# The first product of a gated feed-forward block in seven half-size products, with its result passed through HBM

## The chip, the cores and the metric

One core of one Trainium2 chip runs the whole layer. The metric is the device time of one execution in microseconds; three runs of the kernel before are shown, and one profiled execution of it is read.

## The reference, cut to what matters

The layer is a mixer block (state-space branch and windowed attention, untouched here) and then this, in float32 for 1,024 tokens behind 16 meta tokens:

```python
D_MODEL, D_FF, FFN_CONV = 1024, 2816, 3

def conv_ffn(h, norm_w, w_in, conv_w, conv_b, w_down):
    u = rmsnorm(h, norm_w)
    hid = causal_dwconv(u @ w_in.astype(u.dtype), conv_w, conv_b)   # (T,1024) @ (1024,5632)
    up, gate = jnp.split(hid, 2, axis=-1)
    return (jax.nn.silu(gate) * up) @ w_down.astype(h.dtype)        # (T,2816) @ (2816,1024)

h = h + valid_h * mixer_block(...)
h = h + valid_h * conv_ffn(h, ...)
y = rmsnorm(h, norm_final_w)
```

The convolution looks two tokens back along the sequence, so the first real token needs the last two meta tokens.

## The kernel before

Every large product keeps float32 accuracy by splitting both operands into a high part in TensorE's rounded float32 format and a remainder. The helper `split` (L93 to L95) does this: ScalarE copies the value into the high part, VectorE subtracts it from the value and writes the remainder. One product is then three matmuls per 128-deep slice of the contraction: high by high, high by remainder, remainder by high (L163 to L165 in `gemm_slice`).

Three stages at the end of the program matter here.

**Output projection** (L975 to L992). The nine token blocks are taken in the order 1, 2, 0, 3, 4, 5, 6, 7, 8 (block 0 holds two meta tokens, the others 128 tokens). For each block two PSUM banks of 512 columns take 24 matmuls each (L983 to L985), VectorE adds the residual into `hh` (L991), which stays in SBUF for all blocks, and `norm_T` (L173 to L186) normalises the block: a square with a running sum on ScalarE (L176), a small step on VectorE (L177), a power on GpSimd (L178), a scaling on VectorE (L179), eight transposes on TensorE (L184), and `split` into the two operand tiles `r1h_` and `r1l_` (1,024 deep, 1,040 tokens).

**First product of the feed-forward block** (L999 on). The 5,632 output channels are 44 jobs of 128 channels, a gate job and an up job in turn. Each job runs `gemm` over three token slices of 344, 344 and 342 columns (the list `SLF`), with 8 contraction steps of three matmuls: 72 matmuls. `conv3` (L1008 to L1016) applies the convolution straight from PSUM. The product of gate and up is split on the spot into `ah` and `al` and stays in SBUF. `prep` (L135 to L146) loads and splits the weights of the job two ahead, through the pool `wp` with three buffers `wf` and two each of `wh` and `wl`.

**Second product** (`down`, L1025 to L1058). As soon as three (or two) chunks of 128 channels are ready (list `G`), their part of the second product runs: 16 banks (8 token blocks by 2 halves) with three matmuls of 512 columns per chunk (L1044 to L1046), and VectorE adds each bank to `hh` (L1047). After the last group each block is normalised and stored.

A scheduler sets the order of the instructions on each engine; each engine runs its own list in that order, and the DMAs of this program are all issued from the SP queue, also in order.

## Time and profile before

| | |
|---|---|
| median of 3 runs | 2262.59 us (2261.64 to 2264.21) |
| the profiled execution, its own time | 2263.22 us |
| its span, first to last instruction | 2261.4 us |
| mean granted TensorE clock | 0.996 |
| TensorE busy | 2222.2 us, 98% of the span |
| VectorE, ScalarE, GpSimd busy | 1209.9, 817.7 and 181.5 us |
| start of the first matmul of the first product | 1504.67 us |
| start of the last matmul of the second product | 2254.09 us |

Times inside the span count from its start. Matmuls are pipelined, so the duration of one (0.32 us for 344 columns) is longer than the distance to the next; the distance from start to start is what a stream of them costs. A row of the timeline shows start, duration, engine, line, operation, output from inputs, shape and count, and, where the engine was idle before, for how long and what ended it. Some matmul records are missing from a trace, so stretches are counted by the code and not by the records.

### The profile page before, as it was taken

The page shows a single profiled execution, that of the slowest core. Times are in us where ns is not written, and L with a number is a line of the kernel's source. Part 1 is how long each engine was busy: PE and PEld are TensorE (multiplying, and loading weights), DVE is VectorE, ACT ScalarE, POOL GpSimd, SP SyncE. Part 2 cuts the span into 40 slices and gives each one's busy share as a digit, 9 for nine tenths or more (in the row PEclk, how much of TensorE's full clock was granted, in tenths as well). Part 3 has the DMA queues.
Part 4 walks back from the last instruction along what each step waited for, and adds up shares of the span by engine and source line. Part 5 has one row for each costly group of instructions (what it writes and reads, how often), then busy time and mean ns, then how long its engine had stood idle before and what let it go on. Part 6 is the DMA issues. An engine that isn't in the chain of part 4 may idle for free.

```text
span 2261.4 us, 34124 instructions
## 1 busy us (share of the span) xinstructions
PE 2222.2 (98%) x13546; PEld 2069.9 (92%) x13546; DVE 1209.9 (54%) x2349; ACT 817.7 (36%) x1696; POOL 181.5 (8%) x215
## 2 busy tenths in 40 slices
PE   7999999999999999999999999999999999999998
PEld 6899899998889988989999999789999898989997
DVE  6566554567665465365155545436354544545555
ACT  5445444446543443254222113223132231412333
POOL 1101110003320121031000000000000000000000
PEclk9999999999999999999999999999999999999999
DMA  6522421347643453375355434202020111211112
GB/s 180 121 61 65 112 69 52 96 129 162 153 127 109 131 151 94 95 163 171 100 180 164 116 94 139 97 20 75 19 66 29 56 38 47 63 32 47 57 38 75
DMA packets 286109, 214.38 MB, mean 95 GB/s; under 512 B 29592, under 2 KB 266034, under 8 KB 285439
## 3 DMA queue, kind: packets, MB, share of 16 engines
q1 hardware_dynamic: 285951, 212.21, 33.7%
q8 instruction: 107, 1.75, 0.3%
q14 instruction: 51, 0.42, 0.1%
HBM read 162.42 MB, written 49.74 MB: 94 GB/s over the span
## 4 chain that ended last, share of the span: by engine, by line
PE 92%; DMA 5%; DVE 2%; issue 0%; ACT 0%; SPq 0%; POOL 0%; DVEq 0%; POOLq 0%; ACTq 0%
PE gacc L164 21%; PE gacc L163 21%; PE gacc L165 21%; PE dacc L1044 4%; PE dacc L1046 4%; PE dacc L1045 4%; PE ssdyd L743 2%; PE attO L540 2%; DMA st<-g_d 2%; PE ssdst L730 1%; PE gacc L983 1%; PE gacc L984 1%; PE gacc L985 1%; PE ssdyo L725 1%; DMA att_k<-k_d 1%; PE ssdE L688 1%
## 5 line engine op out<-in xcount | busy, mean ns | idle before, releaser
L163 PE MATMUL gacc<-r1h,wh 128*128 128x342 f32 (+5 forms) x2832 | 919.3, 325 | 6.4 <-DVE cv L449 4.1
L164 PE MATMUL gacc<-r1l,wh 128*128 128x342 f32 (+5 forms) x2832 | 919.6, 325 | 2.2 <-DVE ss L177 1.5
L165 PE MATMUL gacc<-r1h,wl 128*128 128x342 f32 (+5 forms) x2832 | 918.3, 325 | 0.0
L163 PEld LDWEIGHTS gacc<-r1h,wh 128*128 128x128 f32 x2832 | 535.0, 189 | 15.0 <-issue 8.5
L164 PEld LDWEIGHTS gacc<-r1l,wh 128*128 128x128 f32 x2832 | 535.0, 189 | 10.7 <-issue 4.8
L165 PEld LDWEIGHTS gacc<-r1h,wl 128*128 128x128 f32 x2832 | 534.9, 189 | 6.2 <-issue 3.9
L95 DVE TENSOR_TENSOR wl<-wf,wh 128x1024 fp32r<-128x1024 f32 x117 | 144.4, 1234 | 179.2 <-ACT wh L94 177.7
L94 ACT ACTIVATE wh<-wf 128x1024 fp32r<-128x1024 f32 x135 | 142.1, 1053 | 209.8 <-PE gacc L164 183.6
L1047 DVE TENSOR_TENSOR hh<-dacc,hh 128x512 f32<-128x512 f32 x128 | 88.4, 691 | 122.2 <-PE dacc L1046 121.6
L449 DVE SCALAR_TENSOR_TENSOR cv<-gacc,cvw,cv 128x346 f32<-128x346 f32 (+2 forms) x216 | 123.8, 573 | 44.5 <-ACT cv L445 41.4
L1044 PE MATMUL dacc<-dh,ah 128*128 128x512 f32 x352 | 139.1, 395 | 0.0
L1045 PE MATMUL dacc<-dh,al 128*128 128x512 f32 x352 | 139.0, 395 | 0.0
L1046 PE MATMUL dacc<-dl,ah 128*128 128x512 f32 x352 | 139.0, 395 | 0.0
L1012 ACT ACTIVATE cg<-gacc,fcw 128x342 f32<-128x342 f32 (+1 forms) x66 | 41.5, 631 | 258.4 <-PE gacc L165 258.4
L163 PE MATMUL gacc<-r2h,wh 128*128 128x342 f32 x384 | 122.6, 319 | 3.5 <-DVE acc L913 2.4
L165 PE MATMUL gacc<-r2h,wl 128*128 128x342 f32 x384 | 122.8, 320 | 0.0
L164 PE MATMUL gacc<-r2l,wh 128*128 128x342 f32 x384 | 122.8, 320 | 0.0
L1015 DVE SCALAR_TENSOR_TENSOR cg<-gacc,fcw,cg 128x342 f32<-128x342 f32 x132 | 75.3, 572 | 68.4 <-ACT cg L1012 66.5
L1015 DVE SCALAR_TENSOR_TENSOR cu<-gacc,fcw,cu 128x342 f32<-128x342 f32 x132 | 75.4, 571 | 37.4 <-ACT cu L1012 35.3
L1046 PEld LDWEIGHTS dacc<-dl,ah 128*128 128x128 f32 x352 | 66.1, 188 | 16.0
L1044 PEld LDWEIGHTS dacc<-dh,ah 128*128 128x128 f32 x352 | 66.1, 188 | 15.2
L1045 PEld LDWEIGHTS dacc<-dh,al 128*128 128x128 f32 x352 | 66.1, 188 | 15.2
(334 smaller groups left out, 2917.6 us busy)
## 6 DMA issues: line engine op xcount, KB each, us to landing
wf<-in_w_in SPq DMA_DIRECT2D x66, 512.0 KB
wf<-in_w_ffn_in SPq DMA_DIRECT2D x44, 512.0 KB
gl<-ga_d SPq DMA_DIRECT2D x72, 171.0 KB
wf<-in_w_ffn_out SPq DMA_DIRECT2D x22, 512.0 KB
xs_d<-xt SPq DMA_DIRECT2D x16, 520.0 KB
z_d<-zt SPq DMA_DIRECT2D x16, 513.0 KB
ga_d<-gt SPq DMA_DIRECT2D x16, 513.0 KB
st<-g_d SPq DMA_DIRECT2D x48, 171.0 KB
```

What stands on the lines that cost most here:

```text
L94: act.activation(hi, src, AF.Copy)
L95: (eng or dve).tensor_tensor(out=lo, in0=src, in1=ff(hi), op=ALU.subtract)
L163: pe.matmul(ps[:m, :n], wh[:, k, :m], rh[k][:, t0:t0 + n], start=k == 0, stop=False)
L164: pe.matmul(ps[:m, :n], wh[:, k, :m], rl[k][:, t0:t0 + n], start=False, stop=False)
L165: pe.matmul(ps[:m, :n], wl[:, k, :m], rh[k][:, t0:t0 + n], start=False, stop=k == KC - 1)
L449: dve.scalar_tensor_tensor(out=t[:, z:m], in0=ps[:, off + z - lag:off + m - lag], scalar=w, in1=t[:, z:m], op0=ALU.mult, op1=ALU.add)
L540: pe.matmul(O[:, col:col + qn], at.v[:, kb - 1, o:o + P], pts[kb][:, e, q0:q0 + qn], start=False, stop=stop)
L1015: dve.scalar_tensor_tensor(out=t[:, :m], in0=ps[:, off - lag:off + m - lag], scalar=w, in1=t[:, :m], op0=ALU.mult, op1=ALU.add)
L1044: pe.matmul(ps, ah[:, tb], wh[:, cs], start=i == 0, stop=False)
L1045: pe.matmul(ps, al[:, tb], wh[:, cs], start=False, stop=False)
L1046: pe.matmul(ps, ah[:, tb], wl[:, cs], start=False, stop=i == len(grp) - 1)
L1047: dve.tensor_tensor(out=hh[:, b, cs], in0=ps, in1=hh[:, b, cs], op=ALU.add)
```

## The change

The channels of up chunk j and gate chunk j (two 128-channel blocks of the weight) and the two halves of the contraction (512 deep each) form a 2 by 2 block of weights; the two halves of the contraction and the two halves of the tokens (514 and 514 columns, with the two tokens ahead of each half included) form the other 2 by 2 block. Instead of eight half-size products, seven are made from sums and differences of the blocks, in Winograd's form of Strassen's scheme.

The activation sums T1 to T4 are made once, block by block, in the output projection (`sums`): T1 lies in the columns of `r1h_` and `r1l_` that the scheme does not need otherwise, T2 in a new tile, T3 and T4 are stored to HBM (`t_d`) and loaded back afterwards. The blocks are taken in the order 8, 4, 7, 3, 0, 6, 2, 5, 1, since block b and block b + 4 must meet. The residual `hh` no longer stays in SBUF; it is stored to HBM (`h_d`). The weight sums S1 to S4 are made for each j on GpSimd (`wprep`). The product of gate and up is stored to HBM (`a_d`), and the second product is a stage of its own that loads and splits it again (`parts`), with a first group of one chunk and seven of three.

```diff
-    hh = hp.tile([P, NB, D], F32, name="hh")
+    X2 = [xp.tile([P, 4, HT], F32R, name=f"x2{i}") for i in range(2)]
...
+        def sums(t0, n, b11, b21, b12, b22, t3, tz):
...
+            dve.tensor_tensor(out=t1, in0=b12, in1=b11, op=ALU.subtract)
+            split(*col(0, t0, n), b11)
+            split(*col(1, t0, n), b21)
+            dve.tensor_tensor(out=t2, in0=b22, in1=t1, op=ALU.subtract)
+            split(*col(4, t0, n), t2)
+            split(*col(3, t0, n), t1)
+            dve.tensor_tensor(out=t4, in0=b21, in1=t2, op=ALU.subtract)
+            for i, t in enumerate((t3, t4)):
+                z = [q[:, 4 * i:4 * i + 4, :n] for q in tz]
+                split(*z, t)
+                for j in range(2):
+                    sp.dma_start(t_d[i, j][:, :, t0:t0 + n], ff(z[j]))
...
-        for b in [1, 2, 0] + list(range(3, NB + 1)):
+        for b in [8, 4, 7, 3, 0, 6, 2, 5, 1]:
...
-                ht = hh[:, b - 1, :]
+                ht = wp.tile([P, KC, P], F32, tag="wf", name="ht", bufs=3).rearrange("p a b -> p (a b)")
...
-            norm_T(ht, n, t0, wb2, op, ops, "nt")
+            if b > 0:
+                store(h_d[b - 1], ht)
+            nt = [ps for _, ps in norm_ps(ht, n, wb2, op, ops, "nt")]
...
+            elif b > 4:
+                q0 = 2 + P * (b - 5)
+                f2 = wp.tile([P, KC, P], F32, tag="wf", name="f2", bufs=3)
...
+                act.activation(f2[:, K1], nt[0], AF.Copy)
+                act.activation(f2[:, K2], nt[1], AF.Copy)
+                dve.tensor_tensor(out=t3, in0=nt[1], in1=f2[:, K1], op=ALU.subtract)
+                split(*col(2, q0, P), nt[1])
...
+                sums(2 + P * (b - 1), P, nt[0], nt[1], f2[:, K1], f2[:, K2], t3, tz_())
...
-    G = [3, 3, 3, 3, 3, 2, 2, 3]
-    SLF = [(14, 344, 16, 342), (356, 344, 358, 342), (698, 342, 700, 340)]
...
+        X3, X4 = [[fp.tile([P, 4, HT], F32R, name=f"x{i + 3}{j}") for j in range(2)] for i in range(2)]
+        for i, x in enumerate((X3, X4)):
+            for j in range(2):
+                sp.dma_start(ff(x[j]), t_d[i, j])
...
+        SLH = [(0, 258), (258, 256)]
...
+        def wprep(ws):
+            wa, wb = ws
...
+            split(wh, wl, wa)
...
+            pool.tensor_tensor(out=q1[:, K1], in0=wb[:, K1], in1=wb[:, K2], op=ALU.add)
+            pool.tensor_tensor(out=q1[:, K2], in0=q1[:, K1], in1=wa[:, K1], op=ALU.subtract)
+            pool.tensor_tensor(out=q2[:, K1], in0=wa[:, K1], in1=wb[:, K1], op=ALU.subtract)
+            pool.tensor_tensor(out=q2[:, K2], in0=wa[:, K2], in1=q1[:, K2], op=ALU.subtract)
...
+            split(*q1s, q1)
+            split(*q2s, q2)
+            split(*a2, wb[:, K2])
...
+        def product(w, x):
...
+            for t0, n in SLH:
...
+                for k in range(4):
+                    pe.matmul(ps[:, :n], wh[:, k], xh[:, k, xs], start=k == 0, stop=False)
+                    pe.matmul(ps[:, :n], wh[:, k], xl[:, k, xs], start=False, stop=False)
+                    pe.matmul(ps[:, :n], wl[:, k], xh[:, k, xs], start=False, stop=k == 3)
...
+        def conv3(row, c, tag):
+            t = fp.tile([P, SEQ], F32, tag=tag, name=tag)
+            act.activation(t, row[:, 2:2 + SEQ], AF.Identity, bias=fcw[:, 132 + c:133 + c], scale=fcw[:, 88 + c:89 + c])
+            for lag in (1, 2):
...
+                dve.scalar_tensor_tensor(out=t, in0=row[:, 2 - lag:2 - lag + SEQ], scalar=w, in1=t, op0=ALU.mult, op1=ALU.add)
...
+            add("u1", product(w["A11"], B11), None)
+            add("u2", product(w["S2"], T2), "u1")
+            p5 = product(w["S1"], T1)
+            add("u4", p5, "u2")
+            add("u3", product(w["S3"], T3), "u2")
+            fin(rb, 1, p5, "u3")
+            fin(ra, 0, product(w["A12"], B21), "u1")
...
+            fin(rb, 0, product(w["A22"], T4), "u3")
+            tb = conv3(rb, 22 + j, "tb")
+            act.activation(tb, tb, AF.Silu)
+            fin(ra, 1, product(w["S4"], B22), "u4")
+            ta = conv3(ra, j, "ta")
+            dve.tensor_tensor(out=ta, in0=ta, in1=tb, op=ALU.mult)
+            store(a_d[j], ta)
...
+    G = [1, 3, 3, 3, 3, 3, 3, 3]
...
+        def parts(src, slot, first):
+            wf = wp.tile([P, KC, P], F32, tag="wf", name="wf", bufs=3).rearrange("p a b -> p (a b)")
+            sp.dma_start(wf, src)
...
+            split(*t, wf)
...
+                    if gi == 0:
+                        dve.tensor_copy(hh[:, b, cs], ps)
```

`add` copies or adds the two PSUM banks of a product into an SBUF tile `u1` to `u4`, `fin` adds a bank and such a tile into the rows `ra` (up) and `rb` (gate) that the convolution reads: one of the seven products is copied by ScalarE, and the others reach VectorE as 14 additions of one bank.

Three places show how the change moves instructions.

TensorE, at the end of the output projection, before: the transposes (`ntp`) of the last block stand far inside the first slice of the first job, whose tokens do not need that block.

```order
L985 MATMUL gacc<-r2l_11216,r1h 128x512
L983 MATMUL gacc<-r2h_11217,r1h 128x512
L984 MATMUL gacc<-r2h_11217,r1l 128x512
L985 MATMUL gacc<-r2l_11218,r1h 128x512
L163 MATMUL gacc<-r1h,wh 128x344
```

The same place now: the transposes of block 5 stand just ahead of the last two matmuls of block 1, and those of block 1 directly ahead of the first product, with no matmul between.

```order
L1033 MATMUL gacc<-r2h_11220,r1h 128x512
L189 MATMUL ntp<-ident,xn 128x128 x8
L1034 MATMUL gacc<-r2h_11220,r1l 128x512
L1035 MATMUL gacc<-r2l_11221,r1h 128x512
L189 MATMUL ntp<-ident,xn 128x128 x8
L1128 MATMUL gacc<-r1h,wh 128x258
```

So the last block's normalisation now stands between two matmul stretches where it stood beside one.

VectorE at the same place, now (`t_14992` is T3 of block 5 with 1, `t_15097`, `t_15098`, `t_15099` are T1, T2, T4; `ht` is the residual of block 1, `xn` its normalised rows).

```order
L1055 TENSOR_TENSOR t_14992<-ntp,f_14991 128x512
L96 TENSOR_TENSOR r1l<-ntp,r1h 128x4x128
L1041 TENSOR_TENSOR ht<-gacc,ht 128x512 x2
L96 TENSOR_TENSOR wl<-t_14992,wh 128x512
L96 TENSOR_TENSOR wl<-wf,wh 128x1024
L182 TENSOR_SCALAR ss<-ss 128x1
L184 SCALAR_TENSOR_TENSOR xn<-ht,ss,wb_14330 128x1024
L996 TENSOR_TENSOR t_15097<-f_14991,ntp 128x512
L999 TENSOR_TENSOR t_15098<-f_14991,t_15097 128x512
L96 TENSOR_TENSOR r1l<-ntp,r1h 128x4x128
```

The additions for block 1 stand behind work on block 5, and the remainder that the first product reads stands behind T1 and T2.

VectorE at the start of the second product, now (`dacc` are its PSUM banks, `r1l` and `dl` remainders of the loaded chunks).

```order
L1167 TENSOR_TENSOR ra<-gacc,u_20309 128x256
L1145 SCALAR_TENSOR_TENSOR tb<-rb,fcw,tb 128x1024
L96 TENSOR_TENSOR r1l<-wf,r1h 128x1024
L1145 SCALAR_TENSOR_TENSOR ta<-ra,fcw,ta 128x1024 x2
L1185 TENSOR_TENSOR ta<-ta,tb 128x1024
L1239 COPY hh<-dacc 128x512 x4
L96 TENSOR_TENSOR dl<-wf,dh 128x1024 x2
L1239 COPY hh<-dacc 128x512
L1199 TENSOR_SCALAR wbf<-wbf 128x1024
L96 TENSOR_TENSOR dl<-wf,dh 128x1024
L1239 COPY hh<-dacc 128x512 x4
L96 TENSOR_TENSOR r1l<-wf,r1h 128x1024
```

The first copy out of a bank of the second product stands behind the convolution of the last chunk, and the splits of the next chunks stand between the copies.

## Rows read from the trace of the kernel before

**Rows 1.** The page: span, busy time of each engine, the chain that ended last.

```profile
span 2261.4 us, 34124 instructions
PE 2222.2 (98%) x13546; PEld 2069.9 (92%) x13546; DVE 1209.9 (54%) x2349; ACT 817.7 (36%) x1696; POOL 181.5 (8%) x215
...
PE 92%; DMA 5%; DVE 2%; issue 0%; ACT 0%; SPq 0%; POOL 0%; DVEq 0%; POOLq 0%; ACTq 0%
```

**Rows 2.** Timeline of TensorE around the start of the first product.

```profile
1504.67 0.32 PE L163 MATMUL gacc<-r1h,wh 128*128 128x344 f32 x1
...
1512.12 1.03 PE L184 MATMUL ntp<-ident,xn 128*128 128x128 f32 x8
...
1514.14 0.43 PE L164 MATMUL gacc<-r1l,wh 128*128 128x342 f32 x1 [0.30 <-DVE r1l L95]
```

**Rows 3.** Timeline of TensorE, the last matmul of the second product.

```profile
2254.09 0.40 PE L1046 MATMUL dacc<-dl,ah 128*128 128x512 f32 x1
```

**Rows 4.** Timeline of TensorE, first and last of 13 matmuls of the second product.

```profile
1700.18 0.40 PE L1045 MATMUL dacc<-dh,al 128*128 128x512 f32 x1
...
1702.98 0.40 PE L1045 MATMUL dacc<-dh,al 128*128 128x512 f32 x1
```

**Rows 5.** Timeline of TensorE, first and last of 25 matmuls of 272 columns.

```profile
17.57 0.29 PE L165 MATMUL gacc<-r1h,wl 128*128 128x272 f32 x1
...
20.60 0.29 PE L165 MATMUL gacc<-r1h,wl 128*128 128x272 f32 x1
```

**Rows 6.** Groups of instructions of VectorE: count, busy us, mean ns, idle before.

```profile
L95 DVE TENSOR_TENSOR wl<-wf,wh 128x1024 fp32r<-128x1024 f32 x117 | 144.4, 1234 | 179.2 <-ACT wh L94 177.7 <-PE gacc L165 1.4
L1047 DVE TENSOR_TENSOR hh<-dacc,hh 128x512 f32<-128x512 f32 x128 | 88.4, 691 | 122.2 <-PE dacc L1046 121.6
L915 DVE SCALAR_TENSOR_TENSOR gl<-gl,gacc 128x342 f32<-128x342 f32 x48 | 24.5, 510 | 62.7 <-PE gacc L165 62.7
L179 DVE SCALAR_TENSOR_TENSOR xn<-hh,ss,wb 128x1024 f32<-128x1024 f32 x8 | 10.3, 1285 | 5.7 <-POOL ss L178 5.7
```

**Rows 7.** Groups of instructions of ScalarE and GpSimd, same columns.

```profile
L94 ACT ACTIVATE wh<-wf 128x1024 fp32r<-128x1024 f32 x134 | 141.7, 1057 | 208.8 <-PE gacc L164 182.6 <-issue 24.1 <-ACT kh L94 0.9
L94 ACT ACTIVATE r1h<-ntp 128x512 fp32r<-128x512 f32 x32 | 17.5, 595 | 58.6 <-PE ntp L184 58.6
L702 POOL TENSOR_TENSOR xe<-xd,dec 128x512 f32<-128x512 f32 x28 | 30.5, 1089 | 48.4 <-DVE xd L699 48.1
```

**Rows 8.** Timeline of GpSimd and VectorE: one VectorE product beside GpSimd, one alone.

```profile
850.88 1.04 POOL L702 TENSOR_TENSOR xe<-xd,dec 128x512 f32<-128x512 f32 x1 [10.04 <-DVE xd L699]
...
851.33 1.68 DVE L694 TENSOR_TENSOR M<-M,cbm 128x1024 f32<-128x1024 f32 x1
...
867.69 1.23 DVE L694 TENSOR_TENSOR M<-M,cbm 128x1024 f32<-128x1024 f32 x1
```

**Rows 9.** Timeline of the other engines: the last block's normalisation.

```profile
1504.87 0.69 DVE L991 TENSOR_TENSOR hh<-gacc,hh 128x512 f32<-128x512 f32 x1 [0.82 <-PE gacc L985]
1505.64 1.06 ACT L176 ACTIVATE xn<-hh 128x1024 f32<-128x1024 f32 x1 [2.43 <-issue]
...
1507.13 0.54 POOL L178 TENSOR_TENSOR ss<-ss,mhalf 128x1 f32<-128x1 f32 x1 [11.45 <-DVE ss L177]
1507.70 1.29 DVE L179 SCALAR_TENSOR_TENSOR xn<-hh,ss,wb 128x1024 f32<-128x1024 f32 x1 [0.72 <-POOL ss L178]
```

**Rows 10.** Busy time by stretch around an idle stretch (us, engines, PEclk, DMA share, GB/s).

```profile
72.00:76.30 4.30, 0.00 (x0) 0.00 (x0) 0.00 (x0) 0.20 (x1) 0.00 (x0) 0.69 0.90 153
76.30:80.00 3.70, 3.62 (x14) 3.66 (x15) 2.02 (x9) 0.91 (x4) 0.19 (x1) 0.50 0.72 187
80.00:84.00 4.00, 4.00 (x26) 4.00 (x25) 1.13 (x5) 1.87 (x4) 0.76 (x1) 0.95 0.36 90
```

**Rows 11.** DMA view of 1390 to 1520 us in 40 slices.

```profile
GB/s 57 2 169 256 228 316 339 418 412 121 20 305 7 188 268 30 5 0 0 0 0 0 0 0 5 0 0 0 0 0 0 0 0 60 106 0 0 0 0 5
```

**Rows 12.** The chain that ended last: start, us, what; one load of 512 KB.

```profile
652.95 3.42 DMA wf<-in_w_in
```

More of the change, by code (lines that the diff above doesn't have):

```diff
@@ L38 @@
 L_BAND, L_M1, L_M31 = 384, 144, 16
+HT = SEQ // 2 + 2
 AHEAD_BG = 170
@@ new lines, in place @@
+        def place(row, half, s):
+            t0, n = SLH[s]
+            c = 2 if half and s == 0 else 0
+            o = 512 * half + t0
+            return row[:, o + c:o + n], slice(c, n)
+        def conv3(row, c, tag):
+            t = fp.tile([P, SEQ], F32, tag=tag, name=tag)
+            act.activation(t, row[:, 2:2 + SEQ], AF.Identity, bias=fcw[:, 132 + c:133 + c], scale=fcw[:, 88 + c:89 + c])
+            for lag in (1, 2):
+                w = fcw[:, (2 - lag) * 44 + c:(2 - lag) * 44 + c + 1]
+                dve.scalar_tensor_tensor(out=t, in0=row[:, 2 - lag:2 - lag + SEQ], scalar=w, in1=t, op0=ALU.mult, op1=ALU.add)
+            return t
@@ new lines, in body, with add, fin @@
+        w = wprep(wload(0))
+        nxt = wload(1)
+        for j in range(NH):
+            ra = fp.tile([P, SEQ + 2], F32, tag="ra", name="ra", bufs=2)
+            rb = fp.tile([P, SEQ + 2], F32, tag="rb", name="rb", bufs=2)
+            u = {}
+            def add(name, accs, o):
+                u[name] = fp.tile([P, 2, 258], F32, tag=name, name=name)
+                for s, (_, n) in enumerate(SLH):
+                    if o is None:
+                        act.activation(u[name][:, s, :n], accs[s], AF.Copy)
+                    else:
+                        dve.tensor_tensor(out=u[name][:, s, :n], in0=accs[s], in1=u[o][:, s, :n], op=ALU.add)
+            def fin(row, half, accs, o):
+                for s, ps in enumerate(accs):
+                    dst, c = place(row, half, s)
+                    dve.tensor_tensor(out=dst, in0=ps[:, c], in1=u[o][:, s, c], op=ALU.add)
+            add("u1", product(w["A11"], B11), None)
[5 more added lines that the diff above has]
+            fin(ra, 0, product(w["A12"], B21), "u1")
+            if j + 1 < NH:
+                wn = wprep(nxt)
+                if j + 2 < NH:
+                    nxt = wload(j + 2)
+            fin(rb, 0, product(w["A22"], T4), "u3")
[5 more added lines that the diff above has]
+            store(a_d[j], ta)
+            w = wn
@@ L1003, in body @@
+    upx.close()
+    G = [1, 3, 3, 3, 3, 3, 3, 3]
+    with ExitStack() as fs:
+        fp = fs.enter_context(tc.tile_pool(name="dp", bufs=2, reuse_waits="tile"))
+        fps = fs.enter_context(tc.tile_pool(name="dps", bufs=4, space=PSUM))
+        hh = fp.tile([P, NB, D], F32, name="hh", bufs=1)
         wbf = fp.tile([P, D], F32, name="wbf", bufs=1)
@@ L1018, in body @@
[L1018 to L1037 removed]
+        def parts(src, slot, first):
+            wf = wp.tile([P, KC, P], F32, tag="wf", name="wf", bufs=3).rearrange("p a b -> p (a b)")
+            sp.dma_start(wf, src)
+            if first:
+                t = [wp.tile([P, KC, P], F32R, tag=q, name=q, bufs=WB).rearrange("p a b -> p (a b)") for q in ("wh", "wl")]
+            elif slot is not None:
+                t = [r[:, slot, 0:SEQ] for r in (r1h_, r1l_)]
+            else:
+                t = [fp.tile([P, D], F32R, tag="d" + q, name="d" + q, bufs=6) for q in "hl"]
+            split(*t, wf)
+            return t
@@ new lines, in chunks @@
+        def chunks(grp, first):
+            return [(parts(a_d[j], j % KC, first), parts(w2[j * P:(j + 1) * P, :], None, first)) for j in grp]
+        groups, o = [], 0
+        for g in G:
+            groups.append(range(o, o + g))
+            o += g
+        nx = chunks(groups[0], True)
+        for gi in range(len(G)):
+            cur, last = nx, gi == len(G) - 1
+            if not last:
+                nx = chunks(groups[gi + 1], False)
+            for b in range(NB):
+                tb = slice(b * P, (b + 1) * P)
+                if last:
+                    hb = fp.tile([P, D], F32, tag="hb", name="hb")
+                    sp.dma_start(hb, h_d[b])
+                    dve.tensor_tensor(out=hh[:, b], in0=hh[:, b], in1=hb, op=ALU.add)
```

153 lines of the change are left out of this document (85 added, 68 removed).

## The prediction, made before the changed kernel ran

> **What bounds the kernel now.** I read the page first [rows 1]: TensorE is busy for 98% of the span and holds 92% of the chain that ended last, so time is gained where TensorE gets less to do and lost where it is made to wait. Durations of single matmuls overlap, so I price them by the distance from start to start. The two products of the feed-forward block run from 1504.67 us [rows 2] to the last matmul at 2254.09 us [rows 3]; with one more step of 0.23 us that is 749.7 us. In it lie 1,056 matmuls of 512 columns (22 chunks by 16 banks by 3), whose step is (1702.98 - 1700.18) / 12 = 0.2333 us [rows 4], 246.4 us in all. Eight transposes and the waits around them take about 1.1 us [rows 2]. The rest, 502.2 us, are the 3,168 matmuls of the first product (44 jobs by 72), 158.5 ns each. No wait of note stands there: the stage is TensorE's own length.
>
> **The seven products.** A pair of jobs had 144 matmuls of 343.3 columns on average; a pair now has 7 products by 2 slices by 12 = 168 matmuls of 258 or 256 columns. There are more instructions and 43,176 columns in place of 49,440. What a step of 257 columns costs is not in the trace. The nearest row has 272 columns: 24 steps in 20.60 - 17.57 = 3.03 us, 126.25 ns [rows 5], with a new weight tile for each, as here. From 272 to 343.3 columns the step grows by 32.2 ns, 0.45 ns per column; carried on, 257 columns take 119.5 ns. Bounds: 126.25 ns if the step falls no further, and 119.3 ns if it falls in proportion to the columns. I take 119.5, since the three measured widths lie on one line (from 272 to 512 columns it is 0.446 ns per column). A pair then takes 168 by 119.5 = 20.1 us in place of 22.8, and the 22 pairs 441.7 us: **-60.5 us** (bounds -36 and -61).
>
> The Trainium skill (TensorE: Matmul & The Clock Gate, Back-to-back issue gap) gives N/2.4 + 2.5 ns for an isolated stream; for 272 columns that is 115.8 ns, which this trace contradicts. By that rule a step would take 109.6 ns, the term would be -97 us and the time some 2192 us; the measurement decides, and I give that no chance.
>
> **What hides beside them.** Per pair VectorE gets three splits of 1,024 columns at 1.23 us, one of 512 at 0.69, 14 additions out of PSUM of 257 columns, four convolution steps of 1,024 at 1.29 and one product at 1.23 [rows 6]. For the additions, 342 columns take 0.51 us and 512 take 0.69 [rows 6], so 257 take 0.42. The sum is 3.70 + 0.69 + 5.88 + 5.14 + 1.23 = 16.6 us, under the 20.1 us that TensorE needs. ScalarE has about 8 us: six copies or activations of 1,024 at 1.06 and some smaller ones [rows 7]. GpSimd has four sums of 512 at 1.09 us [rows 7]. With eight PSUM banks and slices of 1.43 us, VectorE may be some 5 us late with a bank before TensorE stops, so I cost this at nothing. If the cover is gone, the first rival tells the price. Per pair 1 MB of weights comes in and 0.5 MB goes out, 78 GB/s, where up to 418 GB/s moved [rows 11].
>
> **From output projection to first product.** Before, the last block's normalisation ran beside the first job. Now the first product reads block 1, the last one made. Let 0 be the end of block 1's last matmul. The transposes of block 5 end about 0.5 us before, and behind them ScalarE has four half-block copies (0.60 each, [rows 7]) and VectorE T3 and a remainder (0.69 each), before it adds block 1 out of two banks: done at about 3.0. Then come the square 1.25, VectorE's weight split that is in the way until 4.9, the power 0.54 with its waits to 5.8, the scaling 1.29 to 7.1 [rows 9], the transposes to 7.9, and on VectorE T1, T2 and the remainder (3 by 0.69) to 10.0. TensorE stands still for that long, where before it waited 0.3 us. After an idle stretch of 4.3 us the clock stood at 0.50 for 3.7 us, its lower level, 1.2 GHz, and was back at 0.95 in the next 4 us [rows 10]; so the first product takes some 5 us in place of 2.9 and ends at 15.2.
>
> The second product needs S2. Its second half of the weights goes into a buffer that is free at 7.1; a load takes 3.4 us [rows 12], three GpSimd sums 3.3 us, and ScalarE's copy stands behind another weight copy: high part at 17.8, remainder at 19.2. The products of S2 and S1 end at about 24.1. T3 and T4 come back from HBM: the last store is issued at 13.5, then 4.2 MB are loaded, at some 300 GB/s [rows 11] 7 us for T3 (landed at about 22.7) and 7 more for T4 (29.7), needed at 24.1 and 29.9. So the first pair ends at 35.6 in place of 20.1; less the 1.1 us that the join cost before, **+14.5 us**. Bounds: 8 us, the bare normalisation [rows 9], and 30 us, if T3 and T4 come at half that rate.
>
> **From first to second product.** The second product has the same matmuls as before, but its first group has one chunk: 16 banks of 0.70 us, 11.2 us. It has four PSUM banks, and VectorE's copies stand behind the last chunk's convolution: the last addition is done 0.9 us behind the last product, then come a convolution step 1.29, a split 1.23, two steps 2.57 and a product 1.23, so the first copy starts at about 7.2 us. The sixteenth bank needs the twelfth copy; until that is done VectorE has 12 copies of 0.69, five splits of 1.23 and a small step, together 15.1 us. TensorE ends the group at 7.2 + 15.1 + 0.7 = 23.0 in place of 11.2: **+12 us**. Bounds: 3 us, if splits wait for nothing and go elsewhere, and 20 us, if the loads through three buffers come late too. After that a group of three gives VectorE 16 by 0.69 + 6 by 1.23 = 18.4 us beside 33.6 us of TensorE: nothing.
>
> The output projection keeps its matmuls; a pair of its blocks takes 22.4 us of TensorE and gives VectorE some 13 us: nothing. Its stores and loads stand in order on the SP queue, and each residual block is loaded 4 us or more ahead of its use. The end of the kernel is as before.
>
> **Sum.** Span 2261.4 - 60.5 + 14.5 + 12 = 2227.4 us. The profiled execution lasted 1.8 us longer than its span and 0.6 us longer than the median of the runs: about **2229 us**. A measurement of this kernel can tell about 0.2%, 4.5 us, from no change.
>
> **Rivals.** *VectorE and GpSimd get in each other's way.* One VectorE product took 1.68 us in place of 1.23 where 0.59 us of it lay beside a GpSimd instruction [rows 8], so up to three quarters of the overlap are lost. If all four GpSimd sums fall beside VectorE's two-input work, VectorE needs up to 16.6 + 4.4 = 21.0 us per pair and becomes the bound: 22 by 0.9 = 20 us more, 2249 us. For it: the overlap in rows 8. Against it: VectorE's additions out of PSUM fill a third of its time. Chance 0.18. The Trainium skill states it more sharply (SBUF — State Buffer, SBUF: two separate sides): a VectorE instruction with two SBUF inputs and a GpSimd one that reads SBUF lock each other out for the whole instruction. By that rule the whole 4.4 us would be lost, the rival's time; the one pair in rows 8 agrees in kind, at 0.45 us lost of 0.59.
>
> *The step stops shrinking at 126 ns.* For it: weight loads take their own time beside the matmuls; against: three widths on one line. 22 by 168 by 6.75 ns = 25 us more, 2254 us. Chance 0.04.
>
> *VectorE's chain becomes the bound with every hand-over exposed (slower).* Sums, remainders, convolution and activation pass six times per pair between ScalarE and VectorE, and most of their tiles have one buffer. If each hand-over of 1.06 us stood in VectorE's way, a pair would take 16.6 + 6 by 1.06 = 23.0 us: 22 by 2.9 = 64 us more, 2293 us. It decides for slower from 21.6 us per pair on (33 us over 22 pairs). For it: VectorE idled 178 us in front of splits waiting for ScalarE [rows 6]. Against: that was idle time without need, and each hand-over has several us until TensorE asks for it. Chance 0.12.
>
> *The scheme does not save what it says*: the matmuls are counted above; no chance of its own.
>
> **How the numbers follow.** Forecast 0.66, rivals 0.18, 0.04 and 0.12. The forecast's own spread is from 2212 (every term at its lower bound) to 2252 us (both joins at their upper). The range reaches over the first and second rival and leaves out the slower one and the tails: 2213 to 2258 us. Faster by over 0.2% are the forecast and nearly all of the first two rivals, 0.82; within 0.2% their tails, 0.05; slower 0.13.
>
> **What would show it.** In the profile after: a step of 119 to 120 ns in the first product, 168 matmuls in 20.1 us for a pair in the middle of the stage; TensorE idle for about 10 us ahead of the first product, with a clock of 0.50 behind it; VectorE at 80 to 90% in the stage and TensorE without idle time there; TensorE stopping for PSUM at the start of the second product. A pair of over 20.5 us with TensorE waiting for VectorE would prove the forecast wrong, and so would joins of together over 50 us.

## The result, and the profile of the changed kernel

The changed kernel takes 2233.38 us (median of four runs, 2231.25 to 2233.84), the kernel before, in the same comparison, 2263.40 us (2261.64 to 2264.75). The ratio is 0.9866, with a 95% interval of 0.9849 to 0.9883: 30 us faster, at 2229 us forecast. The profiled execution has a span of 2232.0 us, and all the sums below are made against the 2261.4 us of [rows 1]. Its page (span, busy times, shares of the chain that ended last):

```profile
span 2232.0 us, 35782 instructions
PE 2172.7 (97%) x14074; PEld 2018.5 (90%) x14074; DVE 1364.6 (61%) x2481; ACT 834.4 (37%) x1636; POOL 336.8 (15%) x303
PE 91%; DMA 4%; DVE 3%; ACT 1%; issue 1%; SPq 0%; POOL 0%; DVEq 0%; POOLq 0%; ACTq 0%
```

As in [rows 1], TensorE holds the chain. The timeline of TensorE gives the limits of the stages (in brackets its idle time just before, and what ended it):

```profile
1504.57 0.39 PE L1035 MATMUL gacc<-r2l,r1h 128*128 128x512 f32 x1
1512.46 1.94 PE L189 MATMUL ntp<-ident,xn 128*128 128x128 f32 x8 [7.50 <-DVE xn L184]
1514.95 0.58 PE L1128 MATMUL gacc<-r1h,wh 128*128 128x258 f32 x1 [0.56 <-ACT r1h L95]
1523.77 0.58 PE L1128 MATMUL uacc<-x,q 128*128 128x258 f32 x1 [3.73 <-ACT q L95]
1526.65 0.58 PE L1130 MATMUL uacc<-x,q 128*128 128x258 f32 x1 [0.80 <-DVE q L96]
...
1545.50 0.28 PE L1128 MATMUL gacc<-r1h,wh 128*128 128x258 f32 x1
...
1966.90 0.39 PE L1235 MATMUL dacc<-wh 128*128 128x512 f32 x1
1975.95 0.80 PE L1235 MATMUL dacc<-wh 128*128 128x512 f32 x1 [6.12 <-DVE hh L1239]
...
1990.86 0.39 PE L1235 MATMUL dacc<-dh,r1h 128*128 128x512 f32 x1
...
2224.65 0.40 PE L1237 MATMUL dacc<-dl,r1h 128*128 128x512 f32 x1
```

The output projection ends where it ended before (1504.57 + 0.23 = 1504.80 us; the first product of [rows 2] began at 1504.67). The first pair of the seven products runs from 1514.95 to 1545.50, the other 21 to 1966.90, group 0 of the second product to 1990.86, its other groups to 2224.88. From these rows the balance follows:

- **The products.** 421.40 us / 21 = 20.07 us a pair, and 20.07 / 168 = 119.5 ns a step; before, 502.2 / 22 = 22.83 us a pair. 22 by 2.76 = 60.7 us less.
- **First join.** From 1504.67 to the end of the first pair less one pair is 1545.50 - 1504.67 - 20.07 = 20.8 us; less the 1.1 us of before, 19.7 us more.
- **Second join.** Group 0 takes 23.96 us in place of 48 by 0.2333 = 11.2; the other 1,008 matmuls take 234.0 where 235.2 were to be expected: 11.6 us more.

-60.7 + 19.7 + 11.6 = -29.4 us, the difference of the two spans. The stage itself, away from its ends, is clean. Busy time by stretch in its middle (us, PE, PEld, DVE, ACT, POOL, granted clock, DMA share, GB/s), and groups of VectorE (1515 to 1966 us) and GpSimd (1560 to 1960 us; count, busy us, mean ns, idle before):

```profile
1560.00:1780.00 220.00, 220.00 (x1844) 220.00 (x1844) 183.60 (x257) 84.11 (x99) 79.39 (x46) 1.00 0.25 81
```

```profile
L1162 DVE TENSOR_TENSOR u<-uacc,u 128x256 f32<-128x256 f32 (+1 forms) x83 | 34.1, 417 | 10.7 <-PE uacc L1130 10.7
L1185 DVE TENSOR_TENSOR ta<-ta,tb 128x1024 f32<-128x1024 f32 x21 | 40.0, 1904 | 0.0
```

```profile
L1103 POOL TENSOR_TENSOR q<-wf,q 128x512 f32<-128x512 f32 x19 | 43.2, 2272 | 0.0
L1100 POOL TENSOR_TENSOR q<-wf 128x512 f32<-128x512 f32 x19 | 24.6, 1293 | 84.4 <-DMA wf<-in_w_ffn_in 66.6 <-DVE rb L1167 8.8 <-DVE u L1162 4.5
```

TensorE has no idle time, VectorE is busy for 83%, 183.60 / 220 by 20.07 = 16.75 us of a pair. The additions out of PSUM (L1162) take the 0.42 us that [rows 6] led to. The product of the two branches (L1185) takes 1.9 us in place of 1.23, and a GpSimd sum 1.29 to 2.27: the contention of [rows 8] is there, and under TensorE's time.

The first join is not clean. Stretches of the same view, after the first product begins:

```profile
1514.90:1517.90 3.00, 2.80 (x11) 2.51 (x12) 3.00 (x6) 1.97 (x5) 1.44 (x2) 0.50 0.69 198
1520.90:1523.90 3.00, 0.13 (x1) 0.14 (x1) 0.75 (x1) 2.19 (x3) 1.79 (x2) 0.70 0.95 227
1526.90:1529.90 3.00, 3.00 (x15) 3.00 (x16) 1.26 (x2) 0.00 (x0) 0.00 (x0) 0.50 1.02 430
1532.90:1535.90 3.00, 3.00 (x28) 3.00 (x27) 1.08 (x3) 0.00 (x0) 0.00 (x0) 1.00 1.07 336
```

The clock stands at 0.50, the level of 1.2 GHz, behind the idle time of the norm chain, as in [rows 10]; it comes back (0.87 in 1517.90 to 1520.90), TensorE waits 3.73 us for S2, and it falls a second time, until about 1532: TensorE is then busy without a gap and the view counts 15 matmuls in 3 us, where it counts 28 at full clock (those that reach over an edge included). VectorE's and ScalarE's timelines there show what stood in front of the split of S1 and S2:

```profile
1518.21 1.77 DVE L96 TENSOR_TENSOR wl<-t,wh 128x512 fp32r<-128x512 f32 x1
1524.23 1.22 DVE L96 TENSOR_TENSOR wl<-wf,wh 128x1024 fp32r<-128x1024 f32 x1 [2.58 <-DMA t_d<-wl]
```

```profile
1521.71 1.06 ACT L95 ACTIVATE wh<-wf 128x1024 fp32r<-128x1024 f32 x1 [1.20 <-DVE a L96]
```

At the second join VectorE's timeline shows what stands ahead of group 0's copies (L1239), and ScalarE's the wait in front of it:

```profile
1970.22 1.23 DVE L96 TENSOR_TENSOR r1l<-wf,r1h 128x1024 fp32r<-128x1024 f32 x1 [0.91 <-ACT r1h L95]
1971.36 2.60 DVE L1145 SCALAR_TENSOR_TENSOR ta<-ra,fcw,ta 128x1024 f32<-128x1024 f32 x2
1974.06 1.23 DVE L1185 TENSOR_TENSOR ta<-ta,tb 128x1024 f32<-128x1024 f32 x1
1975.21 2.48 DVE L1239 COPY hh<-dacc 128x512 f32<-128x512 f32 x4
```

```profile
1969.13 1.06 ACT L95 ACTIVATE r1h<-wf 128x1024 fp32r<-128x1024 f32 x1 [2.67 <-DMA wf<-a_d]
```

### The profile page after: what moved, and what is told of

Same layout as the page of the kernel before. It is cut to its first block, busy times and chain, and to the rows that moved or that the text cites. A ratio compares the mean times of both kernels' runs of the same rounds, so it can differ in the third digit from the quotient of the medians.

```text
span 2232.0 us, 35782 instructions
## 1 busy us (share of the span) xinstructions
PE 2172.7 (97%) x14074; PEld 2018.5 (90%) x14074; DVE 1364.6 (61%) x2481; ACT 834.4 (37%) x1636; POOL 336.8 (15%) x303
## 4 chain that ended last, share of the span: by engine, by line
PE 91%; DMA 4%; DVE 3%; ACT 1%; issue 1%; SPq 0%; POOL 0%; DVEq 0%; POOLq 0%; ACTq 0%
PE gacc L169 15%; PE gacc L168 15%; PE gacc L170 15%; PE uacc L1130 4%; PE uacc L1128 4%; PE uacc L1129 4%; PE dacc L1236 4%; PE dacc L1237 4%; PE dacc L1235 3%; PE gacc L1130 2%; PE gacc L1129 2%; PE gacc L1128 2%; PE ssdyd L751 2%; PE attO L548 2%; PE ssdst L738 1%; PE ssdyo L733 1%
## 5 line engine op out<-in xcount | busy, mean ns | idle before, releaser
L168 PE MATMUL gacc<-r1h,wh 128*128 128x342 f32 (+4 forms) x1776 | 581.7, 329 | 5.4 <-DVE cv L457 4.1
L169 PE MATMUL gacc<-r1l,wh 128*128 128x342 f32 (+4 forms) x1776 | 581.4, 328 | 1.8 <-DVE ss L182 1.4
L170 PE MATMUL gacc<-r1h,wl 128*128 128x342 f32 (+4 forms) x1776 | 579.9, 327 | 0.0
L168 PEld LDWEIGHTS gacc<-r1h,wh 128*128 128x128 f32 x1776 | 337.1, 190 | 13.2 <-issue 8.5
L169 PEld LDWEIGHTS gacc<-r1l,wh 128*128 128x128 f32 x1776 | 337.3, 190 | 9.5 <-issue 4.8
L170 PEld LDWEIGHTS gacc<-r1h,wl 128*128 128x128 f32 x1776 | 337.4, 190 | 6.1 <-issue 3.9
L1236 PE MATMUL dacc<-dh,r1l 128*128 128x512 f32 x336 | 133.0, 396 | 0.0
L1237 PE MATMUL dacc<-dl,r1h 128*128 128x512 f32 x336 | 132.5, 394 | 0.0
L1235 PE MATMUL dacc<-dh,r1h 128*128 128x512 f32 x336 | 132.0, 393 | 0.0
L1235 PEld LDWEIGHTS dacc<-dh,r1h 128*128 128x128 f32 x336 | 63.2, 188 | 15.4
L1237 PEld LDWEIGHTS dacc<-dl,r1h 128*128 128x128 f32 x336 | 63.1, 188 | 14.5
```

What stands on the lines that cost most here:

```text
L168: pe.matmul(ps[:m, :n], wh[:, k, :m], rh[k][:, t0:t0 + n], start=k == 0, stop=False)
L169: pe.matmul(ps[:m, :n], wh[:, k, :m], rl[k][:, t0:t0 + n], start=False, stop=False)
L170: pe.matmul(ps[:m, :n], wl[:, k, :m], rh[k][:, t0:t0 + n], start=False, stop=k == KC - 1)
L1235: pe.matmul(ps, ah[:, tb], wh[:, cs], start=i == 0, stop=False)
L1236: pe.matmul(ps, al[:, tb], wh[:, cs], start=False, stop=False)
L1237: pe.matmul(ps, ah[:, tb], wl[:, cs], start=False, stop=i == len(cur) - 1)
```

## Experiments

The theory: the stage is TensorE's own length, the seventh part saved is real, VectorE and GpSimd disturb each other without reaching the end, and 31 us are given back at the two joins. Where a single time is given, it is one execution, and the kernel before took 2262.96 to 2264.09 us beside it. One thing limits small differences: the end of the output projection, ahead of everything that was edited, lies between 1502.2 and 1505.1 us in runs in which its code is the same. The four runs of the changed kernel themselves lie 2.6 us apart. So the parts are compared by their own lengths.

### Eight plain products in the same two stages

```diff
-            add("u1", product(w["A11"], B11), None)
-            add("u2", product(w["S2"], T2), "u1")
...
+            fin(rb, 0, product((w["A21"], B11), (w["A22"], B21)))
+            fin(rb, 1, product((w["A21"], T1), (w["A22"], B22)))
+            fin(ra, 0, product((w["A11"], B11), (w["A12"], B21)))
...
+            fin(ra, 1, product((w["A11"], T1), (w["A12"], B22)))
```

(T1 holds B12 here.)

> The changed kernel with its slices, its way through HBM and its second stage, but with the eight plain half-size products of the standard scheme: two of them are summed in one PSUM bank, 24 matmuls of 258 or 256 columns a slice, and the weight sums, the S splits and the additions out of PSUM are gone (eight copies out of PSUM a pair instead). The token sums are still made and stored, though no product reads T2, T3 and T4. Theory: the step of 119.5 ns belongs to the slice and not to the scheme, so a pair takes 192 x 0.1195 = 22.9 us where the seven products take 20.07, 22 x 2.87 = 63 us more; the wait for the S2 sum at the start falls away, 4 to 8 us. Time 2286 to 2294 us, slower than the kernel before, since both joins stay. Rival, the pair of the seven products is set by VectorE or by the evacuation of the small banks: the pair then grows by less, to 22 us or under, and the time stays under 2270 us.

Measured: 2296.27 us, 33 us slower than the kernel before. Two VectorE products of neighbouring pairs, and TensorE's first product:

```profile
1709.78 1.23 DVE L1159 TENSOR_TENSOR ta<-ta,tb 128x1024 f32<-128x1024 f32 x1
1732.78 1.23 DVE L1159 TENSOR_TENSOR ta<-ta,tb 128x1024 f32<-128x1024 f32 x1
```

```profile
1518.71 0.58 PE L1117 MATMUL gacc<-r1h,q 128*128 128x258 f32 x1 [6.22 <-ACT q L95]
```

A pair takes 23.00 us, 192 steps of 119.8 ns. The narrow slices and the way through HBM give nothing by themselves (22.83 us before): the eighth product alone is what is saved, 2.93 us a pair, 64 us in all. The rival falls. The time is 2 us above the range. The order I chose starts with A21, in the half of the weights that comes last, so that the wait that I had expected to go stood ahead of the first product instead, 6.2 us long.

### GpSimd's weight sums left out

```diff
+            if first:
                 pool.tensor_tensor(out=q1[:, K1], in0=wb[:, K1], in1=wb[:, K2], op=ALU.add)
...
+            else:
+                q1, q2 = wb, wa
```

> Left out: GpSimd's four weight sums from the second pair on; S1 to S4 are then plain halves of the weights, split by the same instructions, so that ScalarE, VectorE and TensorE do as many instructions as in the changed kernel. Theory: GpSimd and VectorE do slow each other down where they run together (in the changed kernel the VectorE product takes 1.98 us instead of 1.22 and a GpSimd sum 2.2 us instead of 1.09), but TensorE sets the pair: the VectorE product falls to 1.2 us, the pair stays at 20.07 us and the time at 2228 to 2235 us. Rival, the contention reaches the end through VectorE: a pair of 19.5 us or less, time 2220 us or less.

Measured: 2231.69 us. The stretch of above, and the VectorE product:

```profile
1560.00:1780.00 220.00, 220.00 (x1844) 220.00 (x1843) 170.47 (x253) 83.58 (x99) 0.00 (x0) 1.00 0.25 80
```

```profile
L1188 DVE TENSOR_TENSOR ta<-ta,tb 128x1024 f32<-128x1024 f32 x15 | 18.3, 1217 | 0.0
```

TensorE does as many matmuls in the stretch (1,844) with GpSimd idle, VectorE needs 15.55 us a pair in place of 16.75, and its product 1.22 us. In the middle of the stage the contention costs VectorE 1.2 us a pair and the kernel nothing. The sums of the first pair stay in this run, so it says nothing of the first join.

### How much more VectorE can take

```diff
             split(*q2s, q2)
+            for t, x, n in (((wh, wl), wa, 1), (q1s, q1, 1), (q2s, q2, 0)):
+                for _ in range(n):
+                    dve.tensor_tensor(out=t[1], in0=x, in1=ff(t[0]), op=ALU.subtract)
```

> Two remainders of 1,024 columns of each pair's weights (that of wa and that of S1 and S2) are computed a second time, with the same operands and the same result: 2 x 1.22 = 2.45 us more for VectorE in each pair. Theory: VectorE is busy for 16.75 us of the pair's 20.07, so 19.2 us still fit under TensorE: the pair stays within 0.1 us of 20.07 and the time within 5 us of 2232 us. Rival, the hand-overs between ScalarE and VectorE have used the slack up already: the pair grows by 1.5 us or more, 32 us in all, time over 2260 us.

The second run has 2, 2 and 1 in place of 1, 1 and 0.

> Five remainders a pair are computed again in place of two (wa's twice, that of S1 and S2 twice, that of S3 and S4 once): 6.1 us more for VectorE. Theory: VectorE now needs 22.9 us and sets the pair, 2.8 us over TensorE's 20.07; over 21 pairs 59 us, time 2285 to 2300 us, with TensorE waiting for VectorE's additions out of PSUM. Rival, the hand-overs between the engines cost more than VectorE's own sum: a pair of 24.5 us or more, time over 2325 us. If the added instructions were hidden (other engines' gaps take them in), the time stays under 2245 us.

Measured: 2233.81 and 2303.09 us. Busy time from 1600 to 1900 us, with two and with five more remainders:

```profile
1600.00:1900.00 300.00, 300.00 (x2513) 300.00 (x2513) 292.00 (x378) 116.38 (x135) 110.63 (x61) 1.00 0.25 80
```

```profile
1600.00:1900.00 300.00, 273.22 (x2174) 264.31 (x2173) 300.00 (x358) 101.90 (x116) 105.75 (x52) 0.99 0.22 68
```

With two, VectorE is busy for 97% of the time and TensorE does not notice. With five, VectorE is busy for all of it, TensorE waits for its additions out of PSUM, and a pair takes 300 / 2174 by 168 = 23.2 us, VectorE's length (22.9 expected; the time is 3 us above the range). So the bound changes between 19.5 us (97% of 20.07) and 22.9 us of VectorE's own work, which fits a change at TensorE's 20.07 us; up to 19.5 us the hand-overs to ScalarE and back do not bring it on.

### A product without a sum ahead of S2, and a useless one in its place

```diff
+            if j == 0:
+                fin(ra, 0, product(w["A12"], B21), "u1")
             add("u2", product(w["S2"], T2), "u1")
...
-            fin(ra, 0, product(w["A12"], B21), "u1")
+            if j > 0:
+                fin(ra, 0, product(w["A12"], B21), "u1")
```

> In the first pair alone A12 x B21 is computed second, ahead of S2 x T2; it needs no weight sum. Theory: at the first join TensorE pays twice for the sum S2 that comes at 1523.8 us, with the wait of 3.7 us and with the clock, which after it stands at 0.50 once more until about 1532.4 (8.6 us at half speed, 4.3 us lost). With A12 x B21 in the gap TensorE keeps going to about 1523 us, the clock stays at 1.00, and the first pair ends some 6.5 us sooner: time 2224 to 2228 us (2232 before). Rival, what follows S2 is what sets the first pair (the remainder of S1 and S2, T3 and T4 from HBM at about 1529): the product saved is waited for elsewhere, and the time falls by less than 2 us.

```diff
+            if j == 0:
+                product(w["A11"], B11)
             add("u2", product(w["S2"], T2), "u1")
```

> In the first pair alone A11 x B11 is computed a second time into a bank that nothing reads, in the place where the run with A12 x B21 moved forward has that product: 24 matmuls more, and no useful work in the gap. Theory: if the falling clock is a price of its own beside the wait, then TensorE does 2.9 us more work and the kernel is still faster, since the clock stays at 1.00 after the gap: 4.3 us back, less some 1.5 us of waiting for the remainder of S1 and S2 that comes at 1526.5 as before: time 2228 to 2230.5 us. Rival, the wait alone counts and the clock recovers as soon as work comes: no gain, 2231 to 2235 us.

Measured: 2229.30 and 2231.37 us. TensorE's timeline and a stretch behind the gap, first with A12 x B21 moved, then with A11 x B11 twice:

```profile
1513.43 0.80 PE L1128 MATMUL gacc<-r1h,wh 128*128 128x258 f32 x2 [0.56 <-ACT r1h L95]
...
1522.31 0.39 PE L1128 MATMUL uacc<-x,q 128*128 128x258 f32 x1 [1.22 <-ACT q L95]
...
1525.54 0.58 PE L1130 MATMUL uacc<-x,q 128*128 128x258 f32 x1 [2.00 <-DVE q L96]
...
1541.38 0.28 PE L1128 MATMUL gacc<-r1h,wh 128*128 128x258 f32 x1
```

```profile
1527.00:1530.00 3.00, 3.00 (x16) 3.00 (x16) 0.43 (x1) 0.00 (x0) 0.00 (x0) 0.50 0.99 417
```

```profile
1524.03 0.38 PE L1128 MATMUL uacc<-x,q 128*128 128x258 f32 x1 [1.24 <-ACT q L95]
...
1526.96 0.39 PE L1130 MATMUL uacc<-x,q 128*128 128x258 f32 x1 [1.71 <-DVE q L96]
...
1543.32 0.28 PE L1128 MATMUL gacc<-r1h,wh 128*128 128x258 f32 x1
```

```profile
1527.00:1530.00 3.00, 3.00 (x25) 3.00 (x26) 1.80 (x3) 0.00 (x0) 0.00 (x0) 1.00 1.02 430
```

The first pair takes 27.95 us with the product moved (1513.43 to 1541.38) and 28.06 us with the useless one (1515.26 to 1543.32), in place of 30.55. The second run does 24 matmuls more, 2.9 us of work, and its first pair is 2.5 us shorter: its clock came through the gap at 1.00. The remainder of S1 and S2 came no sooner, 11.70 us after the first matmul in this run (1515.26 to 1526.96) and in the changed kernel (1514.95 to 1526.65); from there to the end of the pair it took 16.36 in place of 18.85 us. So the falling clock is a price of its own; that theory holds for the pair (4.3 less 1.5 us were expected), though the time came 0.9 us above its range. The first run has the useful order and yet its clock fell again, with 8 matmuls between idle stretches of 1.22 and 2.00 us (1.24 and 1.71 in the other): 2.6 us in place of the 6.5 expected, and a time 1.3 us above its range. What I had left to the rival is the remainder of S1 and S2, which is read 3.2 us behind their high part: VectorE had the second pair's weights in front of it. Why one of two such similar gaps lowers the clock and the other doesn't, these runs don't settle.

### Group 0's copies on two engines

```diff
-                    if gi == 0:
+                    if gi == 0 and 2 * b + half in (0, 1, 2, 3, 6, 8, 10, 12, 14):
+                        cp = act.activation(hh[:, b, cs], ps, AF.Copy).ins
+                    elif gi == 0:
                         dve.tensor_copy(hh[:, b, cs], ps)
...
+                    with tc.issue_after(cp):
+                        x2 += [parts(w2[j * P:(j + 1) * P, :], None, False) for j in (1, 2)]
```

> In the second stage nine of the sixteen copies of group 0 out of PSUM go to ScalarE (the first four, then every second one), the splits of group 1 are put behind the first four copies on ScalarE, and two of its six remainders go to GpSimd. Theory: group 0 takes 23.96 us in place of 11.2 because the first copy stands on VectorE behind the last pair's convolution and product until 1975.2, and the later ones stand between splits; ScalarE is free of the last pair at about 1970.4, so the first copy is done at 1971, TensorE's idle falls from 6.1 us to under 2, the clock does not drop, and group 0 ends 6 to 9 us sooner: time 2223 to 2227 us. Rival, the splits of group 1 that were put back become the wait in place of the copies: TensorE waits at group 1's first bank instead, and the time falls by less than 3 us.

Measured: 2228.53 us, 1.5 us above the range, and group 0 in 18.95 us. VectorE's and TensorE's timelines:

```profile
1977.77 0.69 DVE L1199 TENSOR_SCALAR wbf<-wbf 128x1024 f32<-128x1024 f32 x1 [4.65 <-DMA wbf<-in_norm_final_w]
```

```profile
1970.10 0.50 PE L1243 MATMUL dacc<-wh 128*128 128x512 f32 x1 [0.66 <-ACT hh L1247]
1979.12 0.80 PE L1243 MATMUL dacc<-wh 128*128 128x512 f32 x1 [4.96 <-DVE hh L1249]
```

The first wait fell from 6.12 to 0.66 us, as expected: it came from VectorE's order, since the first four copies, on ScalarE, did not wait. Neither theory had the next wait: a scaling of the final norm's weights, not needed before the last group, stood between two copies and waited for its own load.

### Both joins, one after the other

The last norm's scaling goes behind the last copy:

```diff
-        dve.tensor_scalar(out=wbf, in0=wbf, scalar1=float(math.sqrt(D)), scalar2=None, op0=ALU.mult)
...
+                        if 2 * b + half == 15:
+                            tc.keep_in_program_order(dve.tensor_scalar(out=wbf, in0=wbf, scalar1=float(math.sqrt(D)), scalar2=None, op0=ALU.mult))
```

> The run with the copies of group 0 on two engines, and the scaling of the final norm's weights, 0.69 us of VectorE, behind the last copy of group 0. Theory: in that run the one wait of 4.96 us left at the second join was this instruction, which stood between two copies and waited 4.65 us for its weights from HBM; without it TensorE does not stop for more than 1 us, the clock does not fall (2.4 us lost there), and group 0 takes 12 to 14 us (18.95 with the copies on two engines, 23.96 in the changed kernel): time 2219 to 2223 us. Rival, the third chunk of group 1, whose weights get their buffer only when a remainder of an earlier chunk is done, becomes the wait at group 1's first bank: time 2224 us or more.

And the first join, from the changed kernel:

```diff
+                    if b == 1 and cs is hs[1]:
+                        order1 = os1.enter_context(tc.issue_after(trs[0]))
...
+                tc.keep_in_program_order(s3)
...
+                    with tc.issue_after(w["q"][0]), tc.issue_after(w["q"][1]):
+                        wn = wprep(nxt)
```

> Three orders are changed at the first join, and nothing that is computed: the transposes of block 5 stand on TensorE ahead of the second half of block 1's output projection, so that VectorE is done with block 5 when block 1's additions come; GpSimd makes S1 and S2 of the first pair ahead of S3 and S4, and their split stands on ScalarE and VectorE ahead of the weights of the second pair; and the first pair's products run in the order A11, A12, S2, S1, S4, S3, A22. Theory: with A12 x B21 moved alone the clock fell again, because S2's high part still came 1.2 us and its remainder 2.0 us late behind other splits; both now come before TensorE needs them, so that the first pair takes 22.5 to 24 us (30.55 in the changed kernel, 27.95 with A12 x B21 moved), and its start is some 2 us sooner: time 2222 to 2226 us. Rival, T3 and T4 (from HBM, at about 1527 and 1531 us), or VectorE standing at the second pair's weights until the stores of T4 have landed, take the place of these waits: the first pair stays over 26.5 us and the time over 2227 us.

Measured: 2226.73 and 2228.43 us, 3.7 and 2.4 us above their ranges. ScalarE and SyncE with the scaling later:

```profile
1980.43 1.06 ACT L95 ACTIVATE dh<-wf 128x1024 fp32r<-128x1024 f32 x1 [5.71 <-DMA wf<-in_w_ffn_out]
```

```profile
1971.64 2.47 SPq L1235 DMA_DIRECT2D hb<-h_d  x2
1974.21 0.39 SPq L1203 DMA_DIRECT2D wf<-in_w_ffn_out  x1
```

TensorE did the sixteen banks of group 0 in 13.7 us (1964.75 to 1978.45), then waited 3.42 us at group 1 for the third chunk, whose weights were issued behind 1 MB of residual rows (hb): here the rival was right on the place and the time. Its reason holds only in part: the remainder that frees their buffer, on GpSimd, had ended at 1973.17, 1 us before they were issued, and they then took until 1980.43 behind these rows, 6.2 us where a load took 3.4 [rows 12]. With these rows behind them, in the last run, ScalarE's wait was 2.58 us. With the first join reordered the first pair ran from 1515.67 to 1539.13 with 0.7 us of the second pair's work in it, 22.7 us, as expected; but it began later, not sooner, and TensorE then waited 1.61 us for S2 of the second pair. ScalarE and VectorE there:

```profile
1506.69 1.06 ACT L95 ACTIVATE wh<-wf 128x1024 fp32r<-128x1024 f32 x1 [4.60 <-DMA wf<-in_w_ffn_in]
```

```profile
1507.78 1.22 DVE L96 TENSOR_TENSOR wl<-wf,wh 128x1024 fp32r<-128x1024 f32 x1 [3.06 <-ACT wh L95]
1508.92 0.68 DVE L1047 TENSOR_TENSOR ht<-gacc,ht 128x512 f32<-128x512 f32 x1
```

Block 1's second addition stood behind the split of the first weights, which waited for HBM. The last run mends both and joins them:

```diff
+                with tc.issue_after(trs[1]), tc.issue_after(trs[2]):
+                    split(wh, wl, wa)
...
+                    with tc.issue_after(g1ld):
+                        sp.dma_start(hb, h_d[b])
```

> The orders of both joins together, with two repairs. First join: as in the run with the first join reordered, and the split of the first weights now stands behind block 1's norm on ScalarE and VectorE, since in that run block 1's second addition waited 4.6 us behind it for weights from HBM. Second join: as in the run with the final weights scaled later, and the loads of these weights and of the residual rows stand behind the weights of group 1's third chunk, which in that run landed behind them and held ScalarE for 5.7 us; VectorE takes the remainder that frees that chunk's buffer. Theory: the first product starts some 3 us sooner than in the changed kernel (its norm chain is then the last block's own) and the first pair takes 22.7 us in place of 30.55, about 10 us in all; group 0 takes 12 to 14 us in place of 23.96 and group 1 begins without a wait, another 10 to 12 us: time 2210 to 2216 us, ratio to the kernel before 0.977 to 0.979. Rival, the joins are bound by transfers (T3 and T4, the weights of the second pair, the chunks of group 1 all pass in the same microseconds) and the waits move again: 2218 us or more.

Measured: 2218.81 us, median of five runs (2216.28 to 2220.00); the ratio to the kernel before is 0.9802 with an interval of 0.9788 to 0.9815, which does not touch that of the changed kernel (0.9849 to 0.9883). It beats both. Its TensorE and VectorE timelines:

```profile
1513.15 0.80 PE L1146 MATMUL gacc<-r1h,wh 128*128 128x258 f32 x2 [0.56 <-ACT r1h L95]
1960.43 0.39 PE L1275 MATMUL dacc<-wh 128*128 128x512 f32 x1
1976.25 0.50 PE L1275 MATMUL dacc<-dh,r1h 128*128 128x512 f32 x1 [1.19 <-DVE hh L1281]
```

```profile
1973.77 0.70 DVE L1265 TENSOR_SCALAR wbf<-wbf 128x1024 f32<-128x1024 f32 x1 [3.25 <-DMA wbf<-in_norm_final_w]
```

Against the changed kernel's profile the first product starts 1.8 us sooner (3.2 us sooner after the output projection, which here ended 1.4 us later), the stage from there to group 0 takes 447.28 in place of 451.95 us, and group 0 takes 15.8 in place of 23.96: 1.8 + 4.7 + 8.1 = 14.6 us, where the spans (2217.5 and 2232.0) differ by 14.5. It is less than expected: 2.8 us above the range, in the rival's. At the first join TensorE now waited 1.14 us for T3 from HBM, the first pair took 23.9 us (1513.15 to 1537.40, less 0.36 us of the second pair's work) and not 22.7, and 1.27 us more went into a wait for S2 of the second pair: a part of what the new order gains in the first pair is lost in the next. At the second join VectorE once more stood at the last norm's weights, 3.25 us.

## Why the prediction was right, and where it was off

The forecast was 2229 us, and the likeliest case came; 2233.38 us is inside the range.

**The products: right, -60.7 for -60.5 us.** The step carried on from 272 to 257 columns along the line of the measured widths came out at 119.5 ns. The rival of a step that stays at 126 ns falls. The Trainium skill's formula for isolated matmuls (TensorE: Matmul & The Clock Gate, Back-to-back issue gap), 109.6 ns here, lies 9.9 ns under the measured step, as it lay 10 under that of [rows 5]. The eight plain products show that the scheme itself saves 2.93 us a pair, more than the 2.76 between the two kernels, since narrow slices cost 23.00 us where the old jobs cost 22.83.

**The cover: right, and its size is now known.** I had 16.6 us a pair for VectorE; it is 15.55 without GpSimd's sums and 16.75 with them. The two runs with more remainders put the edge between 19.5 and 22.9 us of VectorE's own work, in keeping with where I had put it, at TensorE's 20.07 us.

**First rival, contention: it exists and did not decide.** I gave it up to 4.4 us a pair. In the middle of the stage it takes 1.2 us from VectorE, since only two of the four sums meet VectorE at work on two SBUF inputs, and GpSimd bears most of it: those two sums take 2.27 us for 1.29. The Trainium skill (SBUF — State Buffer, SBUF: two separate sides) has the two engines lock each other out for whole instructions; the trace agrees in that both get longer where they meet, 2.27 us for 1.29 and 1.90 for 1.22. At the first join it may have reached TensorE: VectorE's split of T4 beside the GpSimd sums took 1.77 us, where 0.68 is usual for 512 columns, and it was for the store of this remainder that VectorE then waited. About 1 us of the late remainder would come from that, by an estimate from these rows; no run leaves out the first pair's sums.

**The slower rival, VectorE's chain with every hand-over exposed: wrong here.** Even at 97% VectorE kept up; a pair of 23.2 us, where that rival had put it, took 6.1 us more of VectorE's own work.

**First join: wait and first fall of the clock right, the size too small, 19.7 for 14.5 us.** The first product began 10.15 us after block 1's last matmul (10.0 forecast) and ran at 0.50. The step that failed is "high part at 17.8, remainder at 19.2. The products of S2 and S1 end at about 24.1": on that clock TensorE read the high part at 19.0 and the remainder at 21.9, and these two products ended at 29.2. The splits stood behind the second pair's weights, whose buffers stores of T4 still read: ScalarE waited 1.20 us there (the trace names another VectorE split, which ended last; in the two runs with a product ahead of S2 it names the store of T4's high part, 1.25 and 1.27 us), VectorE 2.58 us. GpSimd's sums took 1.28 to 1.73 us, not 1.09, but S2 was done at 1521.11, 0.6 us before ScalarE got to these weights. And I let TensorE go on at full speed after a wait of several us, though [rows 10] had shown what idle time does. The second fall held until about 1532. The high part 1.2 us late, the remainder another 1.5 us behind it and 2.5 us for the clock, as the run with the useless product has it, make up the 5.2 us that were missing. The reordered first pair, 22.7 us for 30.55, measures the clock and the waits together, before the 1.61 us that the second pair gave back. T3 and T4, to which I had given the end of the first pair, were not waited for.

**Second join: right, 11.6 for 12 us.** Group 0 took 23.96 us (23.0 forecast), with VectorE's copies behind the last convolution and the first of them 8.3 us after the last product (7.2 forecast). That alone is 12.8 us; the 1.2 us that the later groups gained were in no term of mine, so a part of the agreement is luck. What I had not seen: the tail was itself held by ScalarE's split of a chunk that waited 2.67 us for HBM, and the small step I had counted, the scaling of the last norm's weights, waits for its load when its place comes sooner.

## What to carry to other kernels

A scheme that trades matmuls for additions pays what it removes only as long as the additions stay under TensorE; the sum of VectorE's own instructions against TensorE's length of a pair was the right test here, and adding harmless instructions until the time moves measures the slack. What is lost lies where one stage hands over to the next: there, price the wait, and separately the clock that falls with it, and read each engine's order for work that has no hurry (weights of a later stage, loads of a last group, the next pair's splits) in front of work that TensorE is waiting for. After mending one such wait, look for the next: three of them came up one behind the other at the second join, and at the first the wait for S2 moved on to the next pair.

## What the runs showed that was not expected

24 useless matmuls in a wait made the first pair 2.5 us shorter, because the granted clock stayed at 1.00. Two almost equal gaps, 8 matmuls between idle times of 1.22 and 2.00 us or of 1.24 and 1.71, ended with a fallen clock in one run and not in the other, in one execution each. And VectorE, 97% busy and in two-way contact with ScalarE and GpSimd, held TensorE up at no point in the middle of the stage.
